# Hybrid decoder trunk: the odd tokens' rows and squares by VectorE and column sums instead of TensorE transposes, two pairs' left sums on GpSimd, left operands one group sooner

## The chip, the cores and the metric

One NeuronCore of a Trainium2 chip runs the whole program. The metric is the device time of one execution in microseconds (us); before took 1544.23 us, the median of three runs (1544.19 to 1544.71). Engines: TensorE (PE: matmuls; PEld: its weight loads), VectorE (DVE), ScalarE (ACT), GpSimd (POOL) and SyncE (SP), which only issues DMAs. Each engine executes its own list of instructions in order, and semaphores make one engine wait for another or for a DMA.

## What is computed

One layer on 1024 tokens of 1024 channels in float32:

```
h   = rms_norm(x, g_mix)
...  = h @ w_in                      # conv branch, recurrent branch, gates
ya  = conv branch @ w_a_out ; yb = RG-LRU branch @ w_b_out
m   = sigmoid(ga) * ya + sigmoid(gb) * yb
x1  = x + m @ w_o
h2  = rms_norm(x1, g_mlp)
x2  = x1 + relu(h2 @ w_1)^2 @ w_2    # w_1: 1024 x 4096, w_2: 4096 x 1024
out = rms_norm(x2, g_final)
```

The change lies between `m @ w_o` and the first products with `w_1`: x1 has to be normed (which needs each token's mean square) for the product, and has to be kept with tokens as rows for the last residual sum.

## The kernel before

**Layout.** Activations lie with channels on the 128 partitions and tokens along the free axis. The tokens are split in two halves of 512, "even" (`o` = 0) and "odd" (`o` = 1), and the channels in two halves `kk` (0, 1), each of two tiles `c2`: `x1[kk, o, c2]` is a 128x1024 tile whose two halves of 512 columns (`HALVES`) are two blocks of 128 channels.

**Products.** A float32 product is made as three matmuls of parts: high with high, high with low, low with high. The high part is ScalarE's rounded copy. The low part of a left operand (a block of weights) comes from `split_dma` (L63 to L67): ScalarE writes the negated, rounded block into the tile for the low part, GpSimd issues a DMA that adds the block to it, so that what rounding took off is left, and ScalarE copies the high part. Blocks of two by two are multiplied with seven products instead of eight, in the manner of Strassen: `w_a_out` ("a"), `w_o` ("o") and the first part of `w_1` ("u"). For each product number p there are four groups (pairs i = 0 to 3) of twelve matmuls of 128x512. `gseq` (L1196 to L1198) lists these groups: 28 of "a", 28 of "o" (p in the order 1, 2, 6, 7, 4, 5, 3), then eight of "u" (p = 1 and 2). A slot n of the main loop (L1701) is one such group. The groups are named by pair and product: `gu2_1` is the left operand of "u", pair 2, product 1; its bank is `gu2a`. After the slots the up projection goes on with `up_step` (L1560), whose first group writes `f0b` with the left operand `o0_6` and the right one `gu6`.

**Order of the work.** Every engine's order is that of the Python calls (`manual_schedule`). In slot n the loop calls `g_post` (what follows group n − 1), then `g_mm` (L1266, the twelve matmuls of group n), `g_lhs` (L1249, the left operand of group n + 4), `g_sums`, and what the table `GX` (L1614, L1625, L1643) lists for the slot. VectorE's steps are put into a list with the time from which they are ready (`later`, L696) and come out in that order at the next `vector_work` (L700); `flush` empties the list at once. The times are the planner's (`clk`, `at`), not the chip's.

**Buffers.** `T(name)` hands out one of 37 buffers of 128x1024 in turn: left and right operands of "u", `x1`, the transposed rows `x1r` and raw weights all come from it, and whoever writes a new tile waits until the earlier tile's readers, DMAs among them, are done. `EV` has 14 buffers of 128x512. PSUM's eight banks are one pool (`bank`).

**Squares and rows of x1, even half.** `x1_sq` (L1375): ScalarE squares the eight blocks of 128x512. `x1_add` (L1380): VectorE adds each to the first. `x1_cols` (L1396): four matmuls with a column of ones sum over the partitions, which gives 128 tokens by 4. `x1_turn` (L1385): VectorE transposes 32x32 blocks (two instructions of 128x512 per tile `x1r`), and SyncE stores each tile with four DMAs of 128 KB into `x1d`, an array in DRAM that the down projection reads much later (`x_block`, L1877).

**Odd half.** `x1_rows` (L1404) has TensorE transpose the 32 blocks of 128x128 into PSUM. From there ScalarE squares and sums each row, VectorE copies the rows to a tile, and SyncE stores it with one DMA of 512 KB. This stands in slot u0 = 56, behind the first group of "u".

**Norm, both halves.** `x1_root` (L1434): mean square and ScalarE's square root; `x1_diag` (L1445): VectorE's correction of the root and four diagonal blocks, two by VectorE and two by ScalarE; `x1_spread` (L1458): four matmuls with ones put the factors on all partitions (bank `rbm`); `x1_normed` (L1468): VectorE multiplies x1 by them. `g_parts` (L1208) makes the right operands' parts (`gu1h`, `gu2l`), `g_t` (L1219) differences of right blocks.

**Sums of left blocks.** `up_lhs(i, 6)` (L1510) makes `s1` and `s2` of a pair on VectorE and the left operand of product 6 (`o0_6`) from `s2`.

Of the kernel before, what the change touches and what calls it, by code (L numbers as in the profile page):

```python
# [9 lines left out]
F32 = mybir.dt.float32  # L10
# [5 lines left out]
P = 128  # L16
# [14 lines left out]
def trunk_kernel(ctx: ExitStack, tc: tile.TileContext, x, xt_in, xt_eo, vecs, w_in, w_a_out, w_b_out,  # L31
# [1234 lines left out]
    def g_mm(w, i, p):  # L1266
        b = {1: "a", 2: "a", 6: "b", 5: "e", 3: "e", 7: "f", 4: "f"}[p]
        if p in (1, 5):
            gb[w, i, b] = bank(f"g{w}{i}{b}")
        o, n = go.pop((w, i, p)), 0  # L1270
        for k in range(4):
            h, l = (a[w, p, k // 2][:, HALVES[k % 2]] for a in (gh, gl))
            for a, b_ in ((o[:, 0, k, :], h), (o[:, 0, k, :], l), (o[:, 1, k, :], h)):
                nc.tensor.matmul(gb[w, i, b], a, b_, start=p in (1, 5) and n == 0, stop=n == 11,  # L1274
                                 skip_group_check=p not in (1, 5))
                n += 1
        at("P", 12 * MM)
# [92 lines left out]
    x1d = dp.tile([8, P, D], F32, name="x1d")  # L1370


    sqs = []

    def x1_sq(i, m_):  # L1375
        s = EV(f"sq{i}{m_}")
        nc.scalar.activation(s, x1[i // 2, 0, i % 2][:, HALVES[m_]], AF.Square)
        sqs.append((at("A", 0.62, clk["V"]), s))

    def x1_add(n=1):  # L1380
        for _ in range(n):
            ready, s = sqs.pop(1)
            later(ready, 0.63, tt, sqs[0][1], sqs[0][1], s, ALU.add)

    def x1_turn(kk):  # L1385
        for th in range(2):
            r = T(f"x1r{kk}{th}")
            for c2 in range(2):
                src = x1[kk, 0, c2].rearrange("p (m h b j) -> p h m b j", m=2, h=2, j=32)[:, th]
                dst = r.rearrange("p (b m j) -> p m b j", m=4, j=32)[:, 2 * c2:2 * c2 + 2]  # L1390
                dve(0.65, 0, nc.vector.transpose, dst, src)
            d = x1d[2 * th:2 * th + 2].rearrange("q (b i) (k g x) -> k g i (q b) x", b=4, k=2, g=4)
            for g in range(4):
                nc.sync.dma_start(d[kk, g], r[32 * g:32 * g + 32].rearrange("p (b x) -> p b x", x=P))

    def x1_cols():  # L1396

        sqs.append(bank("cs"))
        for n in range(4):
            nc.tensor.matmul(sqs[1][:, n:n + 1], sqs[0][1][:, n * P:(n + 1) * P], ones[:, 0:1],  # L1400
                             start=True, stop=True)
        at("P", 0.9)

    def x1_rows(*ts):  # L1404
        for t in ts:
            o, n = divmod(t, 4)
            if n == 0:
                rst[o] = cp.tile([P, 6, 4], F32, tag="st6", name=f"stm{o}", bufs=2)
            rows = T(f"x1r{t}")
            for kk in range(2):  # L1410
                ps = bank(f"tr{t}{kk}")
                for c in range(4):
                    nc.tensor.transpose(ps[:, c * P:(c + 1) * P],
                                        x1[kk, o, c // 2][:, c % 2 * HS + n * P:c % 2 * HS + (n + 1) * P],
                                        ident)
                at("P", 0.45)
                a = T(f"sq{t}{kk}")[:, 0:HS]
                nc.scalar.activation(a, ps, AF.Square, accum_out=rst[o][:, kk, n:n + 1])
                at("A", 0.63, clk["P"])

                def copy(rows, kk, ps, t):
                    nc.vector.tensor_copy(
                        rows[:, HALVES[kk]].rearrange("p (g c j) -> p c g j", g=4, c=4),
                        ps.rearrange("p (c g j) -> p c g j", g=4, c=4))
                    if kk:
                        nc.sync.dma_start(x1d[t], rows)

                later(clk["P"], 0.63, copy, rows, kk, ps, t)
            if t == 7:
                x1_root(1)  # L1430
            if o:
                vector_work(clk["V"])

    def x1_root(o):  # L1434

        if o == 0:
            rst[o] = cp.tile([P, 6, 4], F32, tag="st6", name=f"stm{o}", bufs=2)
        a, b, v, s = (rst[o][:, i, :] for i in range(4))
        if o:
            tt(v, a, b, ALU.add)  # L1440
        nc.vector.tensor_scalar(v, v if o else sqs[1][:, 0:4], 1.0 / D, EPS, ALU.mult, ALU.add)
        nc.scalar.activation(s, v, AF.Sqrt)
        at("A", 1.5)

# [65 lines left out]
    def up_lhs(i, p):  # L1510
# [5 lines left out]
                "p (k c) -> p k c", c=P)  # L1516
            return sv[i, n]

        if p == 6:
            s1, s2 = S(1), S(2)  # L1520
            tt(s1, blk(1, 0), blk(1, 1), ALU.add)
# [86 lines left out]
    def flush():  # L1608
        vector_work(clk["V"])

    def g_get(n, f):
        return f(*gseq[n]) if 0 <= n < len(gseq) else None

# [17 lines left out]
        13: ((g_parts, "o", 4, 1),), 14: ((x1_sq, 0, 0),),  # L1631
        15: ((g_parts, "o", 5, 0), (x1_sq, 1, 0)),
        16: ((g_parts, "o", 5, 1), (x1_add,), (x1_sq, 2, 0), (up_load, 0, (0,))),
        17: ((g_parts, "o", 3, 0), (x1_add,), (x1_sq, 3, 0), (x1_sq, 0, 1), (up_load, 1, (0,))),
        18: ((g_parts, "o", 3, 1), (x1_add, 2), (x1_sq, 1, 1), (up_load, 2, (0,))),
        19: ((x1_add,), (x1_sq, 2, 1), (up_load, 3, (0,))),
        20: ((x1_add,), (x1_sq, 3, 1), (flush,), (x1_turn, 0)),
        21: ((x1_add,), (flush,), (x1_cols,), (x1_turn, 1), (up_load, 0, (1,))),
        22: ((x1_diag, 0), (up_load, 1, (1,))),
        23: ((x1_spread, 0), (x1_normed, 0, 0)), 24: ((g_parts, "u", 1, 0), (g_parts, "u", 1, 1)),  # L1640
        25: ((x1_normed, 1, 0),), 26: ((g_parts, "u", 2, 0),), 27: ((g_parts, "u", 2, 1),)}.items()})
    u0 = 2 * o0
    GX.update({u0 + n: v for n, v in {  # L1643
        0: ((up_lhs, 0, 6), (x1_rows, 4, 5, 6, 7)),
        1: ((x1_diag, 1),), 2: ((x1_spread, 1), (up_lhs, 1, 6)),
        3: ((x1_normed, 0, 1), (x1_normed, 1, 1), (g_t, "u", 0, 1), (g_t, "u", 1, 1)),
        4: ((g_t, "u", 0, 2), (g_t, "u", 1, 2)), 5: ((g_parts, "u", 6, 0),),
        6: ((g_parts, "u", 6, 1), (g_parts, "u", 5, 0), (up_lhs, 0, 5)),
        7: ((g_parts, "u", 5, 1), (up_lhs, 1, 5), (g_t, "u", 0, 3), (g_t, "u", 1, 3))}.items()})
    with tc.manual_schedule(engines=ENGINES):  # L1650
# [50 lines left out]
        for n in range(len(gseq) + 1):  # L1701
# [397 lines left out]
```

## Time and profile before

| what | value |
|---|---|
| median of three runs | 1544.23 us |
| profiled execution, its own time | 1544.64 us |
| its span, first to last instruction | 1542.9 us |
| mean granted TensorE clock | 0.999 |
| groups of "u" on TensorE, first to last | 914.91 to 943 us |

Times in the trace count from the start of the span. "Idle before" is the time an engine stood ahead of an instruction, with the engine or DMA that let it go; a row of an issue gives the time from issue to landing.

### The profile page before, as it was taken

What the parts mean: (1) busy time and instruction counts of PE and PEld (TensorE: products, weight loads), DVE (VectorE), ACT (ScalarE), POOL (GpSimd) and SP (SyncE); (2) the same over time, 40 slices, a digit from 0 to 9 for tenths busy, and PEclk for the clock granted to TensorE, in tenths of its full rate; (3) what the DMA queues carried; (4) which work ended last, traced back from release to release, by engine and by line L of the source; (5) the groups of instructions that cost most, each with busy time, mean ns of one, the idle gap of its engine ahead of it and who ended that gap; (6) DMA issues with size and microseconds to landing.
All of it is one profiled execution on the core that took longest, in us unless ns stands there. A gap on an engine that the chain in (4) does not pass through costs nothing.

```text
span 1542.9 us, 19178 instructions
## 1 busy us (share of the span) xinstructions
PE 1533.1 (99%) x6782; PEld 1262.4 (82%) x6782; DVE 1222.5 (79%) x1648; ACT 903.6 (59%) x1261; POOL 184.4 (12%) x219
## 2 busy tenths in 40 slices
PE   9999999999999999999999999999999999999998
PEld 8888788888888888888888887888888888888886
DVE  6899999979899997478569879755555558888897
ACT  6648576567567667345275777554444475555553
POOL 0000000002222222000022332000000001111110
PEclk9999999999999999999999999999999999999999
DMA  8776978898997879953579898333333779888862
GB/s 347 197 189 161 251 187 222 217 280 217 247 253 196 193 191 246 327 157 116 182 201 299 197 193 204 137 122 112 113 114 111 241 216 228 223 222 224 209 130 110
DMA packets 132288, 307.82 MB, mean 200 GB/s; under 512 B 13232, under 2 KB 35248, under 8 KB 132192
## 3 DMA queue, kind: packets, MB, share of 16 engines
q1 hardware_dynamic: 101744, 230.60, 46.0%
q0 software_dynamic: 30304, 75.74, 26.9%
q8 instruction: 53, 0.87, 0.2%
q14 instruction: 43, 0.35, 0.1%
q10 hardware_dynamic: 144, 0.26, 0.0%
HBM read 147.69 MB, written 58.72 MB: 134 GB/s over the span
## 4 chain that ended last, share of the span: by engine, by line
PE 95%; DMA 2%; issue 1%; DVE 1%; SPq 0%; POOL 0%; ACT 0%; POOLq 0%; DVEq 0%
PE z L726 18%; PE d L1863 15%; PE yb L1097 8%; PE e L1983 3%; PE keep L1863 2%; PE z L258 1%; PE rg L534 1%; PE rg L536 1%; PE rg L535 1%; DMA x<-in_x_dram 1%; DMA gu<-w_raw 1%; DMA xc<-in_xt_dram 0%; PE go3f L1274 0%; PE f15d L1550 0%; PE f15c L1550 0%
## 5 line engine op out<-in xcount | busy, mean ns | idle before, releaser
L726 PE MATMUL z<-xh,win_h 128*128 128x512 f32 x400 | 124.9, 390 | 0.0
L726 PE MATMUL z<-xl,win_h 128*128 128x512 f32 x400 | 124.5, 389 | 0.0
L1875 DVE TENSOR_TENSOR acc<-acc,d 128x1024 f32<-128x1024 f32 x72 | 87.8, 1219 | 33.3 <-PE d L1863 32.6
L726 PE MATMUL z<-xh,win_l 128*128 128x512 f32 x400 | 98.2, 391 | 0.0
L726 PEld LDWEIGHTS z<-xh,win_l 128*128 128x128 f32 x400 | 75.1, 188 | 16.9
L726 PEld LDWEIGHTS z<-xh,win_h 128*128 128x128 f32 x400 | 75.0, 188 | 16.7 <-ACT win_h L67 0.7
L637 DVE SCALAR_TENSOR_TENSOR y<-u,vec,y 128x511 f32<-128x511 f32 (+14 forms) x120 | 88.3, 736 | 0.0
L726 PEld LDWEIGHTS z<-xl,win_h 128*128 128x128 f32 x400 | 75.1, 188 | 15.8
L542 ACT ACTIVATE g<-rg,vec 96x1024 f32<-96x1024 f32 x32 | 35.6, 1113 | 85.5 <-issue 46.0
L637 DVE SCALAR_TENSOR_TENSOR y<-yt,csum,y 128x511 f32<-128x511 f32 (+6 forms) x112 | 82.5, 736 | 0.0
L637 DVE SCALAR_TENSOR_TENSOR yt<-u,vec,yt 128x511 f32<-128x511 f32 (+6 forms) x112 | 82.5, 736 | 0.0
L66 POOL DMA_DIRECT2D win_l<-win_raw x25 | 21.8, 871 | 324.3 <-ACT win_l L65 312.3
L1538 ACT ACTIVATE o<-s 128x512 fp32r<-128x512 f32 x56 | 33.7, 623 | 45.7 <-DVE s L1522 26.4
L66 POOL DMA_DIRECT2D zo<-zw x42 | 36.6, 871 | 129.4 <-ACT zo L65 116.1
L1097 PE MATMUL yb<-hgl,wb_h 128*128 128x512 f32 x168 | 51.7, 389 | 0.0
L1097 PE MATMUL yb<-hgh,wb_h 128*128 128x512 f32 x168 | 51.7, 389 | 0.0
L486 DVE SCALAR_TENSOR_TENSOR v<-xb,vec,v 128x1023 f32<-128x1023 f32 (+2 forms) x36 | 46.2, 1282 | 6.9 <-ACT v L477 6.1
L66 POOL DMA_DIRECT2D db_1l<-wr x7 | 6.1, 870 | 310.5 <-ACT db_1l L65 287.9
L1097 PE MATMUL yb<-hgh,wb_l 128*128 128x512 f32 x168 | 41.0, 389 | 0.0
L65 ACT ACTIVATE zo<-zw 128x512 fp32r<-128x512 f32 x42 | 26.3, 625 | 20.7 <-PE z10f L914 2.1
L1063 DVE TENSOR_TENSOR o<-s,o 128x512 fp32r<-128x512 f32 x56 | 37.3, 683 | 0.5 <-ACT o L1538 0.5
L1097 PEld LDWEIGHTS yb<-hgh,wb_h 128*128 128x128 f32 x168 | 31.5, 188 | 6.6
(1805 smaller groups left out, 4669.7 us busy)
## 6 DMA issues: line engine op xcount, KB each, us to landing
w_raw<-in_w_dram SPq DMA_DIRECT2D x34, 512.0 KB, 5.7
fr<-fd SPq DMA_DIRECT2D x32, 512.0 KB, 6.3
wr<-in_w_dram SPq DMA_DIRECT2D x32, 512.0 KB, 6.6
zw<-in_w_in_dram SPq DMA_DIRECT2D x28, 512.0 KB, 6.3
win_raw<-in_w_in_dram SPq DMA_DIRECT2D x25, 512.0 KB, 6.8
win_l<-win_raw POOLq DMA_DIRECT2D x25, 512.0 KB, 6.7
zo<-zw POOLq DMA_DIRECT2D x42, 256.0 KB, 5.6
gates<-zg SPq DMA_DIRECT2D x32, 256.0 KB, 3.9
```

The costliest lines, as they stand in the source:

```text
L65: nc.scalar.activation(l, src, AF.Copy, scale=-1.0)
L66: nc.gpsimd.dma_start(l, src, accum_op=ALU.add)
L486: nc.vector.scalar_tensor_tensor(v[:, d:S], a[:, 0:S - d], cbw_c[:, w * 12 + t:w * 12 + t + 1], v[:, d:S], ALU.mult, ALU.add)
L542: nc.scalar.activation(a, gps.pop((n, gi))[:HD, :], AF.Sigmoid, bias=(ba_c, bx_c)[gi][:, n:n + 1])
L637: nc.vector.scalar_tensor_tensor(o[:, k:], a[:, 0:HS - k], c, o[:, k:], ALU.mult, add)
L726: nc.tensor.matmul(zps[s][:, HALVES[hf]], w[:, k, :], xw[k][part][hf], start=n == 0, stop=n == 23)
L1063: tt(l, src, h.bitcast(F32), ALU.subtract)
L1097: nc.tensor.matmul(ps[hf], a, b[:, HALVES[hf]], start=n == 0, stop=n == len(todo) - 1)
L1538: nc.scalar.activation(o[:, 0], src, AF.Copy)
L1863: nc.tensor.matmul(o, a, b, start=n == 0 and (p != 1 or g == 0), stop=n == len(todo) - 1, skip_group_check=p == 1 and g > 0)
L1875: tt(acc[p, q2], acc[p, q2], ps, ALU.add)
L1983: nc.tensor.matmul(o, a, b, start=n == 0 and t not in LOADED, stop=n == len(todo) - 1, skip_group_check=t in LOADED)
```

## The change

1. The odd half's squares and rows are made as the even half's: `x1_sq`, `x1_add`, `x1_turn` and `x1_cols` take `o`, and `x1_rows` is gone. The odd column sums and the odd spread stand in the middle of a group: before the third of four steps of the first products' `gu1a` and `gu2a` (`G_MID`).
2. The even spread is called one slot sooner, in slot 22 of "o", ahead of the group `go3e`.
3. Pairs 0 and 1's sums `s1` and `s2` are made by GpSimd, called in slot u0 (`up_lhs(i, "sums")`), and both left operands of product 6 in slot u0 + 1.
4. The left operands of "u" are prepared five groups ahead instead of four.
5. The odd half's norm, its second two transposes and the differences `g_t` of the products 1 and 2 are mixed in another order. Three of the eight odd squares lie in halves of two T buffers, which also changes which buffer later tiles get.

```diff
@@ g_mm
         for k in range(4):
+            if k == 2 and (w, p, i) in G_MID:
+                f, *a = G_MID[w, p, i]
+                f(*a)
@@
+    def x1_sq(o, i, m_):
+        n = len(sqt)
+        if o == 0 or 0 < n < 5:
+            s = EV(f"sq{o}{i}{m_}")
+        else:
+            if n in (0, 6):
+                x1_sq.t = T(f"sqs{n}")
+            s = x1_sq.t[:, HALVES[0 if n in (0, 6) else 1]]
+        if o:
+            sqt.append(s)
+        nc.scalar.activation(s, x1[i // 2, o, i % 2][:, HALVES[m_]], AF.Square)
+        sqs[o].append((at("A", 0.62, clk["V"]), s))
...
+    def x1_turn(o, kk, *ths):
+        for th in ths:
+            r = T(f"x1r{o}{kk}{th}")
...
-    def x1_rows(*ts):
...
@@ up_lhs
-        if p == 6:
+        if p == "sums" or p == 6 and (i, 1) not in sv:
+            tt_ = nc.gpsimd.tensor_tensor if p == "sums" else nc.vector.tensor_tensor
             s1, s2 = S(1), S(2)
-            tt(s1, blk(1, 0), blk(1, 1), ALU.add)
-            tt(s2, s1, blk(0, 0), ALU.subtract)
+            tt_(s1, blk(1, 0), blk(1, 1), ALU.add)
+            tt_(s2, s1, blk(0, 0), ALU.subtract)
+            if p == "sums":
+                return
@@
+    G_MID = {("u", 1, 1): (x1_cols, 1), ("u", 1, 2): (x1_spread, 1)}
@@ GX, slots of "o" from 22 on
-        22: ((x1_diag, 0), (up_load, 1, (1,))),
-        23: ((x1_spread, 0), (x1_normed, 0, 0)), 24: ((g_parts, "u", 1, 0), (g_parts, "u", 1, 1)),
-        25: ((x1_normed, 1, 0),), 26: ((g_parts, "u", 2, 0),), 27: ((g_parts, "u", 2, 1),)}.items()})
+        22: ((x1_diag, 0), (x1_spread, 0), (up_load, 1, (1,))),
+        23: ((x1_normed, 0, 0), (x1_sq, 1, 0, 1), (x1_sq, 1, 1, 1)), 24: ((g_parts, "u", 1, 0), (g_parts, "u", 1, 1), (x1_sq, 1, 2, 1)),
+        25: ((x1_normed, 1, 0), (x1_add, 1), (x1_sq, 1, 3, 1)),
+        26: ((g_parts, "u", 2, 0), (x1_add, 1, 2), (x1_sq, 1, 0, 0)),
+        27: ((g_parts, "u", 2, 1), (x1_add, 1), (x1_sq, 1, 1, 0), (x1_sq, 1, 2, 0))}.items()})
@@ GX, slots of "u"
-        0: ((up_lhs, 0, 6), (x1_rows, 4, 5, 6, 7)),
-        1: ((x1_diag, 1),), 2: ((x1_spread, 1), (up_lhs, 1, 6)),
-        3: ((x1_normed, 0, 1), (x1_normed, 1, 1), (g_t, "u", 0, 1), (g_t, "u", 1, 1)),
-        4: ((g_t, "u", 0, 2), (g_t, "u", 1, 2)), 5: ((g_parts, "u", 6, 0),),
+        0: ((up_lhs, 0, "sums"), (up_lhs, 1, "sums"), (x1_sq, 1, 3, 0), (x1_add, 1, 2), (flush,), (x1_turn, 1, 0, 0), (x1_add, 1), (flush,),
+            (x1_turn, 1, 0, 1)),
+        1: ((x1_root, 1), (x1_diag, 1), (up_lhs, 0, 6), (up_lhs, 1, 6)),
+        2: ((x1_normed, 0, 1), (x1_turn, 1, 1, 0, 1), (g_t, "u", 0, 1), (flush,), (x1_normed, 1, 1)),
+        3: ((g_t, "u", 0, 2), (flush,), (g_t, "u", 1, 1)),
+        4: ((g_t, "u", 1, 2),), 5: ((g_parts, "u", 6, 0),),
@@ the loop
-            g_get(n + 4, g_lhs)
+            for d in (4, 5):
+                if n + d < len(gseq) and (gseq[n + d][0] == "u") == (d == 5):
+                    g_get(n + d, g_lhs)
```

More of the change, by code (lines that the diff above doesn't have):

```diff
@@ L1370, in trunk_kernel @@
     x1d = dp.tile([8, P, D], F32, name="x1d")
[L1373 to L1380, printed above, removed]
-        for _ in range(n):
[L1382 to L1387, printed above, removed]
+    sqs = {0: [], 1: []}
@@ new lines, in trunk_kernel, with x1_add @@
+    sqt = []
+    def x1_sq(o, i, m_):
[10 more added lines that the diff above has]
+        sqs[o].append((at("A", 0.62, clk["V"]), s))
+    def x1_add(o, n=1):
+        for _ in range(n):
+            ready, s = sqs[o].pop(1)
+            later(ready, 0.63, tt, sqs[o][0][1], sqs[o][0][1], s, ALU.add)
@@ L1402, in x1_cols @@
         at("P", 0.9)
-    def x1_rows(*ts):
[L1405 to L1432, printed above, removed]
@@ L1434, in x1_root @@
-    def x1_root(o):
[L1436 to L1441, printed above, removed]
+    def x1_root(o):
+        rst[o] = cp.tile([P, 6, 4], F32, tag="st6", name=f"stm{o}", bufs=2)
+        v, s = (rst[o][:, i, :] for i in range(2, 4))
+        nc.vector.tensor_scalar(v, sqs[o][1][:, 0:4], 1.0 / D, EPS, ALU.mult, ALU.add)
```

29 lines of the change are left out of this document (15 added, 14 removed).

## The prediction

> **What bounds the kernel now.** I read the page first: the engines' shares, then the chain that ended last.
>
> ```profile
> span 1542.9 us, 19178 instructions
> PE 1533.1 (99%) x6782; PEld 1262.4 (82%) x6782; DVE 1222.5 (79%) x1648; ACT 903.6 (59%) x1261; POOL 184.4 (12%) x219
> PE 95%; DMA 2%; issue 1%; DVE 1%; SPq 0%; POOL 0%; ACT 0%; POOLq 0%; DVEq 0%
> ```
>
> TensorE is the bound (95% of the chain), so the change is worth what it takes off TensorE in its stage, less the pauses that it makes there. The table by stretches shows the other resources (columns: PE busy, PEld, DVE, ACT and POOL busy, each with its count; granted clock, DMA share, GB/s).
>
> ```profile
> 905.00:910.00 5.00, 5.00 (x24) 4.13 (x23) 5.00 (x7) 4.06 (x6) 0.96 (x2) 1.00 1.01 184
> 915.00:920.00 5.00, 5.00 (x35) 4.48 (x34) 2.56 (x4) 5.00 (x11) 3.08 (x4) 1.00 1.08 249
> 930.00:935.00 5.00, 3.56 (x16) 2.63 (x14) 5.00 (x7) 2.48 (x5) 0.87 (x1) 1.00 1.10 240
> 935.00:940.00 5.00, 4.77 (x21) 3.92 (x22) 4.91 (x6) 3.16 (x5) 0.00 (x0) 1.00 0.45 110
> ```
>
> The stage is crowded: the DMA share is about 1 until 935, ScalarE and VectorE have full stretches, and TensorE stands only about 930 to 936. The waits name that pause: 1.7 us, for the DMA that makes a left operand (`gu`). TensorE's own order of work:
>
> ```profile
> 896.71 0.95 PE L1400 MATMUL cs<-ones,sq 128*128 128x1 f32 x8
> 897.52 0.49 PE L1274 MATMUL go2e<-go5h,go 128*128 128x512 f32 x1
> ...
> 900.38 0.39 PE L1274 MATMUL go3e<-go5h,go 128*128 128x512 f32 x1
> ...
> 914.91 0.39 PE L1274 MATMUL gu0a<-gu1h,gu 128*128 128x512 f32 x1
> 917.63 3.65 PE L1413 MATMUL tr<-ident,x 128*128 128x128 f32 x32
> 921.04 0.48 PE L1274 MATMUL gu1a<-gu1h,gu 128*128 128x512 f32 x1
> ...
> 932.95 0.39 PE L1274 MATMUL gu1a<-gu2h,gu 128*128 128x512 f32 x1
> 935.23 0.74 PE L1274 MATMUL gu1a<-gu2h,gu 128*128 128x512 f32 x2 [1.67 <-DMA gu<-w_raw]
> 937.67 0.39 PE L1274 MATMUL gu2a<-gu2h,gu 128*128 128x512 f32 x1
> 940.39 0.39 PE L1274 MATMUL gu3a<-gu2h,gu 128*128 128x512 f32 x1
> 943.11 0.39 PE L1550 MATMUL f0b<-gu6h,o 128*128 128x512 f32 x1
> ```
>
> A group of twelve matmuls takes 940.39 − 937.67 = 2.72 us. I carry everything to the start of `f0b` (943.11); from there on both kernels issue the same.
>
> **TensorE's own work.** (a) The 32 transposes go: 917.63 to 921.04, −3.41. (b) Four column sums of the odd squares come (middle of `gu1a`); those of the even ones took 896.71 to 897.52: +0.81. (c) The pause: second `gu1a` took 937.67 − 932.95 = 4.72 instead of 2.72, −2.00. It goes because TensorE reaches that group at 936.3 after the waits below (three groups ahead of 944.45), while the operand, issued by 923.9, lands 9.5 us later (row below), at 933.4. Sum −4.60.
>
> **Even spread one group earlier.** It now stands at 900.38, where `go3e` began; its last diagonal block comes from ScalarE:
>
> ```profile
> 900.35 0.70 ACT L1455 ACTIVATE rdm<-ident,stm 128x128 f32<-128x128 f32 x2 [0.29 <-DVE stm L105]
> ...
> 907.96 0.62 ACT L65 ACTIVATE gu<-w_raw 128x512 fp32r<-128x512 f32 x1
> 908.48 0.62 ACT L67 ACTIVATE gu<-w_raw 128x512 fp32r<-128x512 f32 x1
> ...
> 911.79 1.06 ACT L65 ACTIVATE gu2l<-x 128x1024 fp32r<-128x1024 f32 x1 [1.64 <-DVE x L462]
> 912.76 1.04 ACT L67 ACTIVATE gu2h<-x 128x1024 fp32r<-128x1024 f32 x1
> 913.70 0.61 ACT L65 ACTIVATE gu<-w_raw 128x512 fp32r<-128x512 f32 x1
> ```
>
> Block ready at 901.05, needed by the fourth matmul of the spread: I take +0.2 (bounds 0.1 and 0.7, all four blocks waited for or only the last).
>
> **What is late next: ScalarE, held by a buffer.** The T pool hands its 37 buffers round in turn. Counted through the changed program, `gu2_1`'s buffer (left operand of pair 2, product 1) is now the one that `x1r011` had, the last transposed rows of the even half. In before that buffer went to `gu0_2`, much later, and `gu2_1` took the one of the first rows. So ScalarE's copy that opens `gu2_1` waits until the four stores from that buffer have landed. When do they?
>
> ```profile
> 905.35 3.66 SPq L1394 DMA_DIRECT2D x1d<-x1r  x2
> ```
>
> ```profile
> x1d<-x1r SPq DMA_DIRECT2D x1, 128.0 KB, 6.1
> ```
>
> The second row is the last store alone, issued at 907.1 (in the issues of 907 to 909): it lands at 907.1 + 6.1 = 913.2. ScalarE comes to the copy by 908.5 at the latest (907.96, after `gu1h`, plus one square), so it stands about 5 us, and all behind it in its order is late: the odd squares.
>
> ScalarE's list from 913.25 to the last odd square, with pitches from the rows: a left-operand pair 1.04 (907.96 to 908.48, twice), `gu2l` and `gu2h` 1.91 (911.79 to 913.70), a square 0.54:
>
> ```profile
> 892.25 0.63 ACT L1377 ACTIVATE sq<-x 128x512 f32<-128x512 f32 x1 [0.63 <-DVE x L462]
> 892.79 0.61 ACT L65 ACTIVATE go<-wo 128x512 fp32r<-128x512 f32 x1
> ```
>
> Four pairs (`gu2_1`, `gu3_1`, `gu0_2`, `gu1_2`) 4.16, two of `gu2l`/`gu2h` 3.82, four squares 2.16, the last square's end 0.63: 10.77, so 924.0. VectorE has two transposes of the first odd rows in its order ahead of the last add:
>
> ```profile
> 892.67 2.49 DVE L462 STREAM_TRANSPOSE x1r<-x 128x512 f32<-128x512 f32 x4
> ...
> 895.65 0.68 DVE L462 TENSOR_TENSOR sq<-sq,sq 128x512 f32<-128x512 f32 x1
> ...
> 900.29 0.48 DVE L1453 TENSOR_SCALAR rdm<-ident,stm 128x128 f32<-128x128 f32 x2
> ...
> 924.93 0.17 DVE L98 RECIPROCAL stm<-stm 128x4 f32<-128x4 f32 x1
> ```
>
> They cost 2 × 0.62 and start when the add before them is through, at 923.1 (its square ends at 922.4, one pair and a pitch before the last); the last add, 0.68, ends about 924.9, and the column sums start at 924.95. TensorE is there at 914.91 + 0.2 + 2.72 (`gu0a`, no transposes behind it) + 1.36 (half of `gu1a`) = 919.2. **Wait: +5.75.** That takes back what the transposes gave.
>
> **Odd spread** (middle of `gu2a`). TensorE arrives at 924.95 + 0.81 + 1.36 + 1.36 = 928.5. On VectorE after the last add: two transposes 1.24 (926.15), the scaled mean 0.2, then `s4_0`, which needs `s2_0` from GpSimd, 0.68 (927.0), five small steps at 0.17 to 0.2 each (928.0), diagonal blocks 0.70 (928.7); the fourth is needed at about 929.1. No wait, as long as `s2_0` is there by about 926.4.
>
> **The sums on GpSimd.** Four additions of 128x512 move there, which no row of before shows. Nearest rows: the same on VectorE, and the one elementwise form that GpSimd runs, at a quarter of the elements and one input; and a DMA issue:
>
> ```profile
> L1521 DVE TENSOR_TENSOR s<-w_raw 128x512 f32<-128x512 f32 x3 | 2.0, 683 | 0.0
> ```
>
> ```profile
> masks.py:199 POOL TENSOR_SCALAR_AFFINE_SELECT ident<-ident 128x128 f32<-128x128 f32 x1 | 0.3, 282 | 0.0
> ```
>
> ```profile
> 917.55 0.87 POOL L66 DMA_DIRECT2D gu<-w_raw  x1 [0.60 <-ACT gu L65]
> ```
>
> Bounds p = 0.68 (VectorE's) and 2.26 (282 ns × 4 for size × 2 for two inputs); I take 1.13, the affine row by size alone. The sums stand behind `gu1_2`'s issue, which ends about 923.9; `s2_0` comes at 923.9 + 2p = 926.2, in time. At 2.26 it comes at 928.4, and the spread is 1.9 late. [...] VectorE's relief (four times 683 ns) buys nothing by itself: those sums were not ahead of a wait of TensorE.
>
> **Lead of the later operands.** TensorE reaches `f0b` at 943.11 − 4.60 + 0.20 + 5.75 = 944.45; `gu6l` of the first columns is about 0.5 us early by the same adding up. `gu3_2`, the last left operand of this kind, is issued behind the sums and `o0_6`, `o1_6`, at about 932.0. Landing of these DMAs:
>
> ```profile
> DMA to landing us min/median/max: 8.1/9.5/12.4
> ```
>
> ```profile
> go<-wo POOLq DMA_DIRECT2D x4, 256.0 KB, 4.8
> ```
>
> With 9.5 it lands at 941.5, with 12.4 at 944.4, with the uncrowded 4.8 at 936.8; its low part is needed by the third matmul of its group, 944.45 − 2.72 + 0.45 = 942.2: 0 to +2.2; I take +0.7, since the odd rows add eight more stores to this very stretch (16 small ones for four of 512 KB).
>
> Two more operands (`o0_7`, `o1_7`) stand shortly before their use:
>
> ```profile
> o<-s POOLq DMA_DIRECT2D x1, 256.0 KB, 6.9
> ```
>
> ```profile
> o<-s POOLq DMA_DIRECT2D x1, 256.0 KB, 8.2
> ```
>
> Issued at 946.5 and 948.1, they landed about 1 us ahead of use; the traffic of the odd rows' second stores comes just ahead: +0.4 (0 to 1.5).
>
> **Sum:** −4.60 + 0.20 + 5.75 + 0.70 + 0.40 = +2.45. Profiled execution 1544.64 (span 1542.9 and 1.7 around it) + 2.45 = 1547.1; that execution lies 0.41 above the median 1544.23, so against the median **1546.7**, rounded 1546.8.
>
> **Rivals.**
> - *ScalarE isn't held* (the last stores land before ScalarE needs the buffer). The odd squares then end about 5 us earlier, the column sums wait little: −3.41 + 0.81 − 2.00 + 0.2 + 0.4 = −4.0, 1540.2. The step decides at about 910.8: a landing by then costs TensorE no more than the transposes gave. For: even stores issued earlier in the same stretch took 4.2 us in the median. Against: the last one took 6.1 in before, with the DMA share at 1.01.
>
> ```profile
> x1d<-x1r SPq DMA_DIRECT2D x16, 128.0 KB, 4.2
> ```
>
> - *Crowding.* The 16 odd stores fall into 922 to 940 with the left operands; `gu3_2` takes 12.4: 2.2 instead of 0.7, 1548.3. For: the DMA share of 1.08 to 1.10 there. Against: before already stored the same bytes in four pieces.
> - *GpSimd's sums are dear* (slower side): at p = 2.26 the spread waits 1.9, `gu2_2`, issued behind the four sums (9.0 us instead of 4.5), 1.2 more, 0.2 at `gu3_2`: 1546.8 + 2.6 after what overlaps = 1549.4. It decides from p of about 1.4, where `s2_0` passes 926.4 + 0.3 of slack. For: GpSimd's one elementwise row scales to it; VectorE runs without pause beside it. [...]
> - *Nothing changes in effect*: the pause moves, ±0; it lies inside the forecast's spread (1544 to 1547).
>
> **How the numbers follow.** Forecast (ScalarE held, p near 1.1) 0.45, giving 1545 to 1548; crowding 0.20 (1547 to 1549.5); dear sums 0.18 (1547.5 to 1551); not held 0.12 (1539.5 to 1543); rest 0.05. What a measurement of this kernel can tell from no change is 0.2%, 3.1 us: 1541.1 to 1547.3. Faster: not held, 0.12. Same: 0.32 of the forecast, 0.05 of crowding, 0.01 of dear sums and the rest, 0.43. Slower: 0.13 of the forecast, 0.15 of crowding, 0.17 of dear sums, 0.45. The range leaves out not held and the far end of dear sums: 1543.5 to 1550.5.
>
> **What would show it.** Right: in the changed trace, ScalarE stands some 5 us ahead of the copy for `gu2_1`, released by a DMA of `x1d`; TensorE waits 4 to 7 us in the middle of the first `gu1a`, on VectorE's last add; no wait above 0.3 at the even spread; no 1.67 at second `gu1a`. Wrong: ScalarE runs through 908 to 913 (then 1540); a wait at the odd spread with VectorE behind GpSimd (then p is above 1.4); additions on GpSimd under 0.9 or over 1.5 us; a wait over 1 us at `gu3a` on a DMA.

## The result, and the profile after

The changed kernel takes **1552.84 us** (median of four runs, 1552.42 to 1553.09) against 1544.21 us before (1543.59 to 1544.71, four runs): a ratio of 1.0055, 95% interval 1.0039 to 1.0071. It is slower by 8.6 us where 2.5 were forecast, and outside the range. The profiled execution took 1552.89 us. Its page, engine shares and chain:

```profile
span 1551.1 us, 19142 instructions
PE 1534.4 (99%) x6758; PEld 1260.9 (81%) x6758; DVE 1226.3 (79%) x1650; ACT 903.3 (58%) x1253; POOL 188.5 (12%) x223
...
PE 92%; DMA 3%; issue 2%; DVE 1%; ACT 1%; POOL 1%; SPq 0%; POOLq 0%; DVEq 0%; ACTq 0%
```

TensorE's part of the chain fell from 95% to 92%: TensorE has less to do and stands more. Its own timeline shows where (start, length, idle time before and releaser in brackets):

```profile
916.35 0.39 PE L1277 MATMUL gu0a<-gu1h,gu 128*128 128x512 f32 x1
...
919.07 0.39 PE L1277 MATMUL gu1a<-gu1h,gu 128*128 128x512 f32 x1
...
927.07 1.84 PE L1414 MATMUL cs<-ones,sqs 128*128 128x1 f32 x8 [6.47 <-DVE sqs L462]
928.77 0.77 PE L1277 MATMUL gu1a<-gu1h,gu 128*128 128x512 f32 x1
...
931.47 0.63 PE L1277 MATMUL gu2a<-gu1h,gu 128*128 128x512 f32 x1
...
935.39 0.40 PE L1277 MATMUL gu3a<-gu1h,gu 128*128 128x512 f32 x1
...
949.01 0.39 PE L1535 MATMUL f0b<-gu6h,o 128*128 128x512 f32 x1
```

The 32 transposes are gone: `gu1a` comes one group (2.72) behind `gu0a`. Then TensorE stands 6.47 us in the middle of `gu1a`, for VectorE's last add of squares, where the forecast had a wait of 5.75. What was not forecast is seen in the lengths behind it: the column sums take 1.7 us (0.81 for the even ones), and a matmul has a pitch of 0.43 instead of 0.23. The stretches give the reason (the column after POOL's is the granted clock):

```profile
920.00:925.00 5.00, 0.59 (x3) 0.17 (x1) 2.74 (x6) 5.00 (x9) 2.52 (x4) 1.00 1.05 191
925.00:930.00 5.00, 2.93 (x11) 2.77 (x12) 4.16 (x9) 1.68 (x4) 4.84 (x5) 0.52 1.00 182
930.00:935.00 5.00, 5.00 (x23) 4.12 (x23) 2.85 (x8) 3.29 (x8) 3.40 (x4) 0.80 0.94 203
```

**The granted clock fell to half.** A mean of 0.52 and then 0.80 is 4.8 + 2.0 = 6.8 us at half speed, in one piece: the clock is 0.50 in every 0.2 us from 925.2 to 932.0, and 1.00 in the rest of the stage up to 925.0 and from 932.2 on. It began while TensorE still stood, some 1.9 us before the column sums, so about 4.9 of the 6.8 us met TensorE at work and cost it half of that, 2.5 us. Why VectorE's add was late stands on ScalarE:

```profile
908.10 0.62 ACT L1390 ACTIVATE sq<-x 128x512 f32<-128x512 f32 x1
914.28 0.63 ACT L65 ACTIVATE gu<-w_raw 128x512 fp32r<-128x512 f32 x1 [5.57 <-DMA x1d<-x1r]
...
924.34 0.61 ACT L1390 ACTIVATE sqs<-x 128x512 f32<-128x512 f32 x1
```

ScalarE stands 5.57 us ahead of `gu2_1`'s copy for the stores into `x1d`, and the last odd square comes at 924.34 (forecast: ends at 924.0). On VectorE and GpSimd beside it:

```profile
923.70 0.69 DVE L462 TENSOR_TENSOR sqs<-sqs,sqs 128x512 f32<-128x512 f32 x1
924.31 1.30 DVE L462 STREAM_TRANSPOSE x1r<-x 128x512 f32<-128x512 f32 x2
925.53 1.39 DVE L462 TENSOR_TENSOR sqs<-sqs,sqs 128x512 f32<-128x512 f32 x1
...
929.95 1.03 DVE L102 TENSOR_TENSOR stm<-stm 128x4 f32<-128x4 f32 x1
```

```profile
924.77 1.59 POOL L1504 TENSOR_TENSOR s<-w_raw 128x512 f32<-128x512 f32 x1
926.44 1.61 POOL L1505 TENSOR_TENSOR s<-s,w_raw 128x512 f32<-128x512 f32 x1
```

While GpSimd adds, VectorE's add of the same shape takes 1.39 instead of 0.69, and a step of 128x4 takes 1.03 instead of 0.16; the two transposes, with one input, keep their 0.62 to 0.65 each. TensorE's waits in the stage:

```profile
PE cs L1414 <- DVE sqs L462: 6.5, 1, 6.5
PE f1d L1535 <- DMA o<-s: 0.5, 1, 0.5
PE f0d L1535 <- DMA o<-s: 0.4, 1, 0.4
PE f0d L1535 <- DVE gu7l L1063: 0.2, 1, 0.2
```

The small waits at `f0d` and `f1d` are for the left operands of product 7. The one at `f1d` goes back in part to VectorE, which stood for one of the five small buffers (tag `s`) that hold sums and differences of left blocks:

```profile
954.88 0.69 DVE L1509 TENSOR_TENSOR s<-w_raw,s 128x512 f32<-128x512 f32 x1 [0.90 <-DMA o<-s]
```

**The account.** I measure the stage from the first matmul of `go0e` with `go5h` (before 891.27, after 892.36) to the first of `f0c` with `gu3h` (959.43, 967.39), and give how much later a group starts than in before's trace, counted from the stage's start. The ends of the stage, first before and then after:

```profile
891.27 0.39 PE L1274 MATMUL go0e<-go5h,go 128*128 128x512 f32 x1
...
959.43 0.39 PE L1550 MATMUL f0c<-gu3h,o 128*128 128x512 f32 x1
```

```profile
892.36 0.39 PE L1277 MATMUL go0e<-go5h,go 128*128 128x512 f32 x1
...
967.39 0.39 PE L1535 MATMUL f0c<-gu3h,o 128*128 128x512 f32 x1
```

| up to the start of | after | what came in |
|---|---|---|
| second `go0e` (product 3) | +0.47 | even spread sooner (+0.35 is left at `gu0a`) |
| first `gu1a` | −3.06 | transposes −3.41 |
| first `gu2a` | +6.52 | wait 6.64 by start times, column sums 0.81, half clock 2.2 |
| first `gu3a` | +6.91 | half clock 0.3 more, spread without a wait |
| `f0b` | +4.81 | before's pause of 2.0 gone |
| second `f0c` | +6.87 | late operands at `f0d` and `f1d` |

Ahead of the stage, where both kernels have the same instructions in the same order, the changed one is 1.09 us later; behind it nothing more comes up to the last matmul. 6.87 + 1.09 make the 7.96 between the last matmuls; the spans differ by 8.2.

### The profile page after: what moved, and what is told of

The parts are those of the page before. It is cut to its first block, busy times and chain, and to the rows that moved or that the text cites. A ratio compares the mean times of both kernels' runs of the same rounds, so it can differ in the third digit from the quotient of the medians.

```text
span 1551.1 us, 19142 instructions
## 1 busy us (share of the span) xinstructions
PE 1534.4 (99%) x6758; PEld 1260.9 (81%) x6758; DVE 1226.3 (79%) x1650; ACT 903.3 (58%) x1253; POOL 188.5 (12%) x223
## 4 chain that ended last, share of the span: by engine, by line
PE 92%; DMA 3%; issue 2%; DVE 1%; ACT 1%; POOL 1%; SPq 0%; POOLq 0%; DVEq 0%; ACTq 0%
PE z L726 16%; PE d L1857 15%; PE yb L1097 8%; PE e L1977 3%; PE keep L1857 2%; PE z L258 1%; PE rg L534 1%; PE rg L536 1%; PE rg L535 1%; DMA yd<-y 1%; DMA x<-in_x_dram 1%; DMA zo<-zw 0%; DMA o<-s 0%; DMA xc<-in_xt_dram 0%; PE go3f L1277 0%
## 5 line engine op out<-in xcount | busy, mean ns | idle before, releaser
L1097 PEld LDWEIGHTS yb<-hgl,wb_h 128*128 128x128 f32 x168 | 31.5, 188 | 6.6
```

The source lines that it names most:

```text
L1097: nc.tensor.matmul(ps[hf], a, b[:, HALVES[hf]], start=n == 0, stop=n == len(todo) - 1)
```

## The experiments

For each kernel: the median, the stage (as in the table, against before's trace, from one profiled execution), the offset ahead of the stage, TensorE's wait at the odd column sums, and the time at half clock that began in that wait or soon behind it (twice what the mean clock of the stretches lacks to 1, times their length).

| kernel | median us | ratio to before, 95% interval | stage | ahead | wait | half clock |
|---|---|---|---|---|---|---|
| changed | 1552.84 | 1.0055 [1.0039, 1.0071] | +6.87 | +1.09 | 6.5 | 6.8 |
| e1 TensorE kept at work | 1551.42 | 1.0046 [1.0031, 1.0061] | +5.31 | +1.17 | 0.5 | 0 |
| e2 other buffer | 1548.12 | 1.0026 [1.0016, 1.0036] | +2.34 | +1.54 | 3.0 | 3.4 |
| e3 sums on VectorE | 1550.73 | 1.0043 [1.0028, 1.0058] | +5.17 | +0.02 | 5.8 | 6.8 |
| e4 even spread back | 1548.22 | 1.0024 [1.0014, 1.0034] | +1.85 | +0.60 | 2.8 | 3.4 |
| e5 = e4 with e3 | 1546.55 | 1.0017 [1.0008, 1.0026] | +0.21 | +0.70 | 2.0 | 0 |
| e6 before, parts 3 and 4 | 1546.12 | 1.0016 [1.0006, 1.0025] | −0.58 | +0.76 | – | 0 |
| e7 before, part 4 | 1545.91 | 1.0018 [1.0009, 1.0027] | +0.49 | +1.40 | – | 0 |
| e8 = e5, transposes later | 1546.07 | 1.0016 [1.0006, 1.0025] | +0.35 | +0.35 | 1.5 | 0 |
| e9 = e5, product 7 sooner | 1551.51 | 1.0041 [1.0027, 1.0054] | +7.36 | +0.10 | 2.7 | 6.8 |
| e10 control | 1543.62 | 0.9999 [0.9990, 1.0008] | −1.29 | +0.21 | – | 0 |
| e11 = e9, four ahead | 1552.12 | 1.0049 [1.0036, 1.0062] | +7.16 | +0.65 | 2.1 | 6.8 |
| e12 = e8, product 7 sooner | 1546.14 | 1.0014 [1.0005, 1.0023] | +1.22 | +0.41 | 1.5 | 3.4 |
| e13 = e9, more buffers | 1546.38 | 1.0018 [1.0010, 1.0027] | +2.26 | +0.09 | 2.1 | 6.8 |

Before itself was 1543.7 to 1543.9 in these comparisons.

The last two columns hold for the one profiled execution only. Every profiled execution without half clock in the stage has a mean clock over the whole span of 0.999 or 1.0, every one with it 0.995 to 0.998. All executions of a kernel, profiled or not, have that mean on record, and within one kernel it differs: in e5 it was 0.999 in three of ten executions, in e8 in five of ten, in e12 in five of eleven. So a 0 in the last column doesn't say that a kernel always keeps its clock.

**e1: TensorE kept at work.** In `x1_cols(1)`, ahead of the column sums:

```diff
+        if o:
+            for _ in range(27):
+                nc.tensor.matmul(sqs[1][1], gh["u", 1, 0][:, 0:P], gh["u", 1, 0][:, HALVES[0]],
+                                 start=True, stop=True)
```

> The changed kernel with 27 extra matmuls of 128x512 on TensorE ahead of the odd column sums (their result is overwritten), so that TensorE works instead of standing 6.5 us; everything else as in the changed kernel (1552.8 us). Theory (the pause itself lowers the granted clock): column sums start within 0.5 us of 927.1 as before, but the granted clock stays 1.00 in 925 to 935 instead of 0.52 and 0.80, the column sums take 0.8 instead of 1.7 us, the second half of gu1a 1.36 instead of 2.7; gu3a starts about 2.3 us earlier; part of it is given back behind VectorE at f0d and f1d: 1550.5 to 1552. Rival (the half clock is not due to the pause, or costs nothing because VectorE sets the end): clock still 0.5 there, or 1552.8 within 0.5.

```profile
925.00:930.00 5.00, 4.51 (x24) 3.54 (x23) 5.00 (x6) 1.75 (x4) 4.84 (x5) 1.00 1.00 180
930.00:935.00 5.00, 3.73 (x21) 2.94 (x20) 3.44 (x12) 3.16 (x8) 3.40 (x4) 1.00 0.94 205
```

```profile
PE rbm L1448 <- DVE rdm L1438: 1.3, 1, 1.3
```

The clock stays 1.00 where it was 0.52 and 0.80, and `gu2a` starts 1.9 us sooner in the stage (+4.63 for +6.52). All four executions have a mean clock of 0.999, the changed kernel's four 0.996. So here the clock fell with the pause and held without it, and the time is in the theory's range. Most of that goes again at once: the odd spread now waits 1.3 us for VectorE's diagonal blocks, which the slow matmuls had hidden, and at `gu3a` 0.6 is left (+6.28 for +6.91) of the 2.3 expected. At the end of the stage it is 1.6, 1.4 in the median. That the rest comes from VectorE's list being through sooner fits the trace, where VectorE no longer stands for a small buffer ahead of product 7, but no run shows it alone.

**e2: another buffer for `gu2_1`.** The stores of the even rows of `kk` = 1 are called two slots later:

```diff
+            if (o, kk) == (0, 1):
+                held.append((d, r))
+            else:
+                x1_store(d, kk, r)
...
-        24: ((g_parts, "u", 1, 0), (g_parts, "u", 1, 1), (x1_sq, 1, 2, 1)),
+        24: ((g_parts, "u", 1, 0), (g_parts, "u", 1, 1), (x1_sq, 1, 2, 1), (x1_held,)),
```

> The changed kernel with the stores of the even rows of kk=1 called two slots later (SyncE's order changes only by these eight stores going behind the loads of w1_1 and w1_3), so that their two buffers come free later and gu2_1 gets another. Theory (ScalarE's stand for the buffer sets TensorE's pause): ScalarE's stand of 5.57 us ahead of gu2_1 is gone, TensorE's wait at the odd column sums falls from 6.5 to between 0.5 and 2.5 us, the granted clock stays 1.00, and the time is 1545 to 1547.5. Rival one (GpSimd's sums beside VectorE) and rival two (crowded DMAs or too much work on VectorE): the wait stays above 4 us and the time above 1550.

ScalarE no longer stands for `x1d`, and the stage falls by 4.5 us: this is the largest single cost of the change. The wait fell less than expected, the clock still fell, for 3.4 us, and the median, 1548.12, lies above the theory's range. ScalarE's stand ahead of the same copy is shorter, not gone; for what it waits there the profile doesn't name:

```profile
911.24 0.63 ACT L65 ACTIVATE gu<-w_raw 128x512 fp32r<-128x512 f32 x1 [2.08 <-issue]
```

```profile
PE cs L1426 <- DVE sqs L462: 3.0, 1, 3.0
```

```profile
920.00:925.00 5.00, 1.99 (x14) 1.52 (x13) 4.90 (x7) 3.43 (x7) 3.76 (x4) 1.00 1.08 204
925.00:930.00 5.00, 5.00 (x18) 3.73 (x18) 3.99 (x10) 1.52 (x5) 3.68 (x4) 0.66 0.98 186
```

The column sums start at 924.03 here, and the mean up to 925 is still 1.00: this time the clock fell at least 1 us after TensorE was at work again.

**e3: the sums of pairs 0 and 1 on VectorE.**

```diff
-        0: ((up_lhs, 0, "sums"), (up_lhs, 1, "sums"), (x1_sq, 1, 3, 0), ...
+        0: ((x1_sq, 1, 3, 0), ...
```

> The changed kernel with the sums s1 and s2 of pairs 0 and 1 back on VectorE (as part of the left operand of product 6), everything else as changed. Theory: the sums only lengthen VectorE's last add (1.39 us beside GpSimd, 0.69 alone), so the column sums start about 0.7 us sooner and the half clock remains: 1551.5 to 1552.5; VectorE pays 2.7 us for them after the diagonal blocks, which may take the gain back. Rival (GpSimd's sums are the main cost): TensorE's wait falls below 3 us, 1546 to 1548.

The wait falls by the forecast 0.7 (6.5 to 5.8), but the stage by 1.7 and the median by 2.1, to 1550.73, between the two ranges. VectorE's steps behind the column sums are shorter too: the step of 128x4 takes 0.16 again. GpSimd's sums are a cost, and not the main one. This trace also shows the clock fall inside a pause, in a stretch without a single matmul:

```profile
920.00:925.00 5.00, 0.00 (x0) 0.00 (x0) 2.99 (x5) 5.00 (x10) 1.84 (x3) 0.86 1.03 188
```

**e4: the even spread back behind `go3e`.**

```diff
-        22: ((x1_diag, 0), (x1_spread, 0), (up_load, 1, (1,))),
-        23: ((x1_normed, 0, 0), ...
+        22: ((x1_diag, 0), (up_load, 1, (1,))),
+        23: ((x1_spread, 0), (x1_normed, 0, 0), ...
```

> The changed kernel with the even spread back in the slot behind go3e. Theory: the earlier spread cost TensorE about 0.5 us (go3e starts 1.56 us later by the shift that is left after it, 1.09 ahead of it), which the later wait swallows, so the time is within 0.7 of 1552.8; the even norm on VectorE starts 1.4 us later. Rival (the earlier spread gains or costs more than 1 us): 1551.5 or less, or 1554 or more.

The theory falls, and the rival's lower half holds by far: 4.6 us faster. ScalarE does not stand for `x1d`. It opens the same copy right behind the square ahead of it:

```profile
908.57 0.61 ACT L1390 ACTIVATE sq<-x 128x512 f32<-128x512 f32 x1
909.09 0.62 ACT L65 ACTIVATE gu<-w_raw 128x512 fp32r<-128x512 f32 x1
```

```profile
x1d<-x1r SPq DMA_DIRECT2D x1, 128.0 KB, 6.6
```

The second view is the last even store, issued after 909, so it landed no sooner than 915.6. A copy at 909.09 can't have waited for it: `gu2_1` has a buffer other than that of `x1r011`. (The trace has no buffer numbers; this is how far it shows it.) The calls of `T` stand in the same order in both kernels, since the spread takes a PSUM bank and no T buffer. So the buffers are not handed out simply in turn, as the text ahead of the prediction and the prediction had it; who gets which hangs on the order of other calls too, and how is open here. Part 2 of the change, which was worth nothing on TensorE, brought on the stand. e2 and e4 take it away by different means and end within 0.1 us of each other in the median.

**e5: e4 and e3 together.** The diffs are those two.

> The changed kernel with the even spread back behind go3e (which gives gu2_1 another buffer, so that ScalarE does not stand) and the sums of pairs 0 and 1 back on VectorE. Against the run with the spread back alone (1548.2, wait at the odd column sums 2.8 us). Theory (GpSimd's additions lengthen VectorE's steps beside them: last add 1.40 instead of 0.69, s4 1.63, one small step 1.03 instead of 0.16): the last add takes 0.69 again, the wait falls to about 2.1, from the column sums' end to the diagonal blocks 2 us instead of 3.6; 1545.5 to 1547.5. Rival (those steps are off the path, and the sums back on VectorE delay the odd norm): 1548 to 1549.5.

```profile
921.08 0.65 DVE L462 TENSOR_TENSOR sqs<-sqs,sqs 128x512 f32<-128x512 f32 x1
```

```profile
PE cs L1414 <- DVE sqs L462: 2.0, 1, 2.0
PE f1d L1535 <- DMA o<-s: 0.7, 1, 0.7
PE f0d L1535 <- DMA o<-s: 0.6, 1, 0.6
```

In e4 that add took 1.40. The wait is 2.0 as expected, the clock stays 1.00 in this execution, and 1.7 us are gained in the median. The three executions with a mean clock of 0.999 took 1544.95 to 1545.87, the seven with 0.997 or 0.998 took 1546.04 to 1547.97. Up to `f0b` this kernel is 2.34 us ahead of before's trace, and gives it back at `f0d` and `f1d`.

**e6: before with parts 3 and 4 of the change** (sums on GpSimd, left operands five groups ahead), rows and spread as in before.

```diff
+            for d in (4, 5):
+                if n + d < len(gseq) and (gseq[n + d][0] == "u") == (d == 5):
+                    g_get(n + d, g_lhs)
...
+        0: ((up_lhs, 0, "sums"), (up_lhs, 1, "sums"), (x1_rows, 4, 5, 6, 7)),
+        1: ((x1_diag, 1), (up_lhs, 0, 6), (up_lhs, 1, 6)), 2: ((x1_spread, 1),),
```

> The kernel before with two parts of the change alone: left operands of the up part five groups ahead, sums of pairs 0 and 1 on GpSimd. Rows and squares of the odd half stay with TensorE, the even spread stays where it was. Theory (the odd column sums wait for a chain over ScalarE and VectorE that the transposes' 3.4 us covered): no wait of TensorE over 1 us in 890 to 945, the old pause of 1.67 us gone or smaller, 1542 to 1544.5. Rival (the earlier left operands or GpSimd's sums are what costs): TensorE waits over 2 us there, above 1546.

No wait at column sums, since there are none; TensorE waits 0.9 us at the odd spread, for VectorE. Its trace loses 1.19 us more far behind the stage, in the down projection, 0.9 of it in one wait for VectorE; why is open. The waits are the theory's, but the median, 1546.12, is above the theory's range and just over the rival's 1546.

**e7: before with part 4 alone** (the first block of e6's diff).

> The kernel before with one part of the change alone: left operands of the up part prepared five groups ahead instead of four. Theory: the operand gu1_2, whose DMA ended the pause of 1.67 us, is issued about one group (2.7 us) sooner, so the pause goes and nothing else moves: 1542.0 to 1543.2. Rival (the traffic is the bound, the operand lands no sooner, or VectorE takes the pause over): 1543.7 to 1545.

The rival holds, and more: 2.1 us slower. The pause at the second `gu1a` is gone, but TensorE waits 1.13 in the transposes for VectorE, and that goes back to a load:

```profile
919.44 0.69 DVE L1521 TENSOR_TENSOR s<-w_raw 128x512 f32<-128x512 f32 x1 [2.24 <-DMA w_raw<-in_w_dram]
```

In before this step ran at 915.71 without a wait. The two loads issued between 895 and 920 took 10.4 us to land in the median where they took 7.7 in before:

```profile
w_raw<-in_w_dram SPq DMA_DIRECT2D x2, 512.0 KB, 10.4
```

```profile
w_raw<-in_w_dram SPq DMA_DIRECT2D x2, 512.0 KB, 7.7
```

That the sooner left operands take the loads' bandwidth is argued, not shown.

**e8: e5 with the first odd transposes behind the last add**, the next two behind the diagonal blocks, and pair 1's sums behind the first half of the norm.

```diff
+        0: ((x1_sq, 1, 3, 0), (x1_add, 1, 3), (flush,), (x1_turn, 1, 0, 0)),
+        1: ((x1_root, 1), (x1_diag, 1), (x1_turn, 1, 0, 1), (up_lhs, 0, 6)),
+        2: ((x1_normed, 0, 1), (up_lhs, 1, 6), (x1_turn, 1, 1, 0, 1), ...
```

> The changed kernel with the even spread back, the sums on VectorE (pair 0 behind the odd diagonal blocks, pair 1 behind the first half of the odd norm), and the first two odd transposes behind the last add instead of ahead of it, the next two behind the diagonal blocks. Theory: the last add ends about 1.3 us sooner than with the spread back and VectorE's sums alone, so the wait at the odd column sums is under 1 us, the granted clock stays 1.00; VectorE's work from there to product 7 is the same, so some of it returns at f0d: 1544 to 1546.5. Rival (VectorE sets the end of the stage whatever the order): within 0.5 of the run with the spread back and the sums on VectorE.

The wait is 1.5, not under 1, and `f0b` starts 2.86 us ahead; the end is that of e5, as the rival has it (1546.07 for 1546.55, which is in the theory's range too). TensorE now also waits at `f0b` for VectorE:

```profile
PE f0b L1535 <- DVE gu6l L1063: 0.8, 1, 0.8
```

**e9: e5 with the left operands of product 7 sooner.**

```diff
-        6: ((g_parts, "u", 6, 1), (g_parts, "u", 5, 0), (up_lhs, 0, 5)),
-        7: ((g_parts, "u", 5, 1), (up_lhs, 1, 5), ...
+        6: ((g_parts, "u", 6, 1), (g_parts, "u", 5, 0), (up_lhs, 0, 5), (up_lhs, 0, 7)),
+        7: ((g_parts, "u", 5, 1), (up_lhs, 1, 5), (up_lhs, 1, 7), ...
...
-    ready = 4
+    ready = 6
```

> As the run with the even spread back and the sums on VectorE (1546.55), with the left operands of product 7 (pairs 0 and 1) prepared in the slots of product 5 instead of in the first slot of the up projection. There TensorE was 2.3 us ahead of the kernel before at f0b and gave it back at f0d and f1d, waiting for those operands (0.6 and 0.7 us to the first low part, more to the others), which ScalarE reached only at 946.9. Theory (with the column sums' wait small, the next late thing is ScalarE's order behind the norm): f0d and f1d wait under 0.5 us together, the stage ends 1 to 2.3 us sooner: 1544.3 to 1545.6. Rival (VectorE sets it: gu7l late instead): within 0.5 of 1546.5.

Wrong on both sides, 5 us slower, and instructive: VectorE stood for one of the five small buffers, and TensorE behind it.

```profile
951.00 0.69 DVE L1509 TENSOR_TENSOR s<-w_raw,s 128x512 f32<-128x512 f32 x1 [3.00 <-DMA o<-s]
```

```profile
PE f0c L1535 <- DVE gu5l L1063: 3.2, 1, 3.2
```

The clock fell a second time behind that wait of 3.2 us, for another 3.4 us:

```profile
955.00:960.00 5.00, 4.13 (x11) 3.33 (x12) 5.00 (x6) 5.00 (x8) 1.74 (x2) 0.66 1.08 256
```

Of the five executions, one had a mean clock of 0.999 and took 1548.20; the others, at 0.995 and 0.996, took 1550.28 to 1552.37.

**e10: a control**, before with a memset of 128x4 on VectorE near the end.

```diff
+    nc.vector.memset(rst[1][:, 0, :], 0.0)
     gfin = T("gfin")
```

> The kernel before with one VectorE memset of 128x4 added near its end, off the path. The changed kernels' traces lie 0.0 to 1.5 us behind the trace of before at the start of this stage, although the instructions up to there are the same. Theory A (it is chance from run to run, or hangs on any change of the program): this kernel's runs lie 0.3 us or more above 1543.85, or spread wider than before's 1543.2 to 1545.6. Theory B (it belongs to the change): within 0.2 of before.

```profile
PE gu1a L1274 <- DMA gu<-w_raw: 0.3, 1, 0.3
```

The time is that of before (1543.62 for 1543.83 in the same comparison), with none of theory A's signs and 0.01 outside theory B's bound; the offset ahead of the stage is 0.21. Its trace shows something else: the pause at `gu1a` that I credited with 2.0 us is 0.3 here, with the same instructions up to that point. So its length is a matter of the execution, and I had read it from one.

**e11: e9 with left operands four groups ahead** (`d == 4` in the loop).

> As the run with product 7's left operands sooner, with the left operands of the up part four groups ahead again, as in before. Theory (the early operands put ScalarE's 1.04 us per pair ahead of the odd squares): the odd squares and the last add end 1 us sooner, the wait at the odd column sums is under 1.2 us instead of 2.0; the second products' operands land later, and a pause of up to 1.7 us like before's may come back: 1543.5 to 1545.5. Rival (the operands' lead is what TensorE needs): 1545.5 to 1547.

The theory falls on the wait: it is 2.1 at the column sums, as in e13 with five ahead. On the time the run is inconclusive, since VectorE stands for a small buffer as in e9, and TensorE behind it at `f0c` (3.5 us): 1552.12, outside both ranges.

**e12 and e13: product 7 sooner without the lack of buffers**, e12 on e8 and e13 on e9:

```diff
+            if i < 2:
+                sv[i, 3] = M(f"s3_{i}")[:, 0:HS].rearrange("p (k c) -> p k c", c=P)
+            tt(sv[i, 3] if i < 2 else S(3), blk(0, 0), blk(1, 0), ALU.subtract)
```

> As the run with the odd transposes moved behind the last add (1546.1; 2.9 us ahead of before at the start of f0b, all of it given back at f0b, f0d and f1d), with the left operands of product 7 prepared in the slots of product 5 and the difference s3 in a buffer of the 12 of 128x1024, since with the five small buffers VectorE stood 3.0 us for one of them. Theory (what takes the gain back is the lateness of product 7's left operands): f0d and f1d wait under 0.6 us together, the stage ends 1 to 2 us ahead of before's trace, 1543.0 to 1545.0. Rival (VectorE's order sets the end, gu6l and gu7l then): f0b and f0d wait over 1.5 us for VectorE, 1545.5 to 1547.

> As the run with product 7's left operands sooner (1551.5), with s3 in a buffer of the 12 of 128x1024 instead of the five small ones; the order on every engine is that run's. Theory (that run lost 5 us to VectorE's stand of 3.0 us for a small buffer, and the granted clock's fall behind TensorE's pause at f0c): the stand and the pause at f0c are gone, the clock falls at most once, at the odd column sums, 1544.5 to 1547. Rival (the order itself, product 7 ahead of gu5, is what costs): f0c still waits over 2 us for gu5l, above 1549.

e13 confirms that e9's loss was the buffer: no wait at `f0c`, 5.1 us faster than e9. In both the waits at `f0d` and `f1d` are gone, and no time is won by it: 1546.14 for e8's 1546.07, 1546.38 for e5's 1546.55. In e12 they are replaced:

```profile
PE f0b L1537 <- DVE gu6l L1063: 1.4, 2, 0.8
```

The traces of e12 and e13 alone can't settle it, because the clock fell in them and not in those of e8 and e5. At a mean clock of 0.999, though, five executions of e12 took 1545.36 to 1546.09 and five of e8 1545.35 to 1546.44. So the late operands of product 7 were not what held the rest. VectorE's list between the odd spread and `gu6l` is the likely cause: in e12 VectorE is busy all but 0.04 of these 10 us (4.96 and 5.00 in the rows).

```profile
930.00:935.00 5.00, 5.00 (x23) 4.13 (x23) 4.96 (x9) 2.77 (x6) 1.08 (x2) 1.00 1.01 180
935.00:940.00 5.00, 5.00 (x23) 4.13 (x22) 5.00 (x8) 1.72 (x3) 0.00 (x0) 1.00 0.99 213
```

No run took that work away, so this is not shown. No version of the change that was tried beats the kernel before.

## Why the prediction was wrong

The way to the main wait was foreseen; what failed is the assumption that TensorE's clock holds behind it, and two terms were too small. Term by term:

- **Transposes −3.41**: measured −3.41, exactly the step as put.
- **ScalarE held by `x1r011`'s stores**: right in place, releaser and size (5.57 us, "about 5"; copy at 914.28, forecast 913.25 plus the 1.09 of the offset). e2 and e4 show that it carries 4.5 to 5.0 us of the stage, by the wait and the clock behind it. That the count of buffers in turn pointed at the right one was luck: e4 has the same order of `T` calls and no stand.
- **Wait +5.75 at the column sums**: 6.64 by start times. The term was mis-sized where I gave the last add 0.68: GpSimd ran beside it, and it took 1.39. (By the prediction's own figures that add ends at 925.0 and not 924.9, which changes little.) The rival on GpSimd's sums asked only whether `s2_0` would come late, not what the sums do to VectorE's own steps. e3, and e5 against e4, price that at 1.6 to 1.7 us of the stage, the clock behind the wait included. Only some of those steps were longer beside GpSimd: the add 1.39 for 0.69, while a transpose took 0.65 for 0.62.
- **The odd column sums at +0.81 and all matmuls at full pitch**: this is the step that failed outright. It took the granted clock as 1.00 through the stage, as in before, where the longest pause of the stage was 1.7 us. From inside the pause of 6.5 us on it was 0.5 for 6.8 us, which cost TensorE 2.5 us on the way to `gu3a`; with the clock kept at 1.00, e1 ends the stage 1.6 us sooner. Half clock lasted 3.4 us in e2 and e4 and 6.8 in the changed kernel; what sets its length no run shows.
- **Even spread +0.2**: +0.35, in its bounds. That it also settles which buffer `gu2_1` gets (e4) was not seen.
- **Pause at `gu1a` −2.0**: gone, as put, but its length in before differs by execution (0.3 in e10's trace). Against e10's trace the gain is smaller by about 1.4; which of the two is usual, two traces don't tell.
- **Odd spread, no wait**: right by luck; the slow matmuls ahead of it hid VectorE's lateness, and with full clock it waits 1.3 (e1).
- **GpSimd's additions at 1.13**: 1.27 to 1.61, past the 1.5 that the prediction named as a sign of being wrong.
- **`gu3_2` +0.7**: no wait; the left operands landed in 4.3 us in the median (3.8 to 7.8) instead of 9.5. **`o0_7`, `o1_7` +0.4**: 2.06 from `f0b` to the second `f0c`, the other mis-sized term. VectorE had four transposes and the odd norm ahead of it, and stood 0.90 for a small buffer; how the 2.06 divides is open.

Sum of the terms as measured: −3.41 + 0.81 + 0.35 + 6.64 + 2.5 − 2.0 + 2.06 = 6.95; the stage shows 6.87. Against the forecast 2.45 the clock accounts for 2.5, the wait for 0.9, product 7 for 1.7, the spread for 0.15, and `gu3_2` takes 0.7 back: 4.5 of 4.4. The other 1.1 of the profiled executions' distance lie ahead of the stage. Over all traces that offset was between 0.0 and 1.5 us, and 0.2 in the control. What sets it is open.

The prediction's last step, from 1546.7 to "rounded 1546.8", is a slip of 0.1.

As a cause of the loss against before: the stand for the buffer 4.5 to 5.0 of the stage (with its half clock), 4.6 to 4.7 in the medians; GpSimd's sums 1.6 to 1.7, and 1.7 to 2.1 in the medians. What is left in e5 is 0.2 against before's trace, 1.5 against the control's, and 2.7 in the median, where seven of ten executions lost clock; the three that kept it lie 1.1 to 2.0 above before's 1543.85. Part 4 alone showed a loss of that size (e7: +0.49, 1.8 above the control's, 2.1 in the median). That it is the same loss is argued, not shown.

## What to carry to other kernels

When work moves to another place in a hand-written order, follow the buffers as well as the engines: a call one slot sooner gave a tile another buffer, and an in-order engine stood 5.6 us for that buffer's old stores. Price a pause of TensorE with the clock that it can cost behind it (here 2.5 us behind a pause of 6.5), and an addition on GpSimd with what it does to VectorE's steps beside it (an add of 1.39 us for 0.69). A wait seen in one profiled execution is worth what it is in several, and so is a clock that held; look at a second trace, and at the mean clock of all executions, before crediting either.

## What the runs showed of the hardware

- In the traces the granted clock fell in or soon behind pauses of 2.1 us (e11, e13), 2.7 (e9), 2.8 (e4), 3.0 (e2), 5.8 (e3) and 6.5 (changed kernel), and of 3.2 at `f0c` (e9; in e11, which paused 3.5 there, the mean clock over the span was 0.995 too); it held behind 1.7 (before) and 2.0 (e5). Behind 1.5 it held in e8 and fell in e12. With one program it held in some executions and fell in others (e5: mean clock 0.999 in three of ten, 0.997 or 0.998 in seven). The pause can be shorter than the time at half clock: 1.5 and 3.4 us in e12, 2.1 and 6.8 in e11 and e13.
- GpSimd's addition of 128x512 in float32 took 1.27 to 1.61 us beside VectorE (changed kernel), against 0.69 for VectorE alone; VectorE's own took 1.39 beside it.
- The last even 128 KB store of transposed rows took 6.1 us to land, before and after. GpSimd's DMAs of 256 KB for the left operands took 3.8 to 7.8 us in after (median 4.3) where they took 8.1 to 12.4 in before (median 9.5); why is open.
